# Where the low parts of u are made in an MLP's down projection, and how many of its pairs take seven products

## The chip, the cores and the metric

The kernel runs on one core of one Trainium2 chip. The metric is the device time of one execution in microseconds (us); the median of three runs of the kernel before is 1048.01 us. Five engines take part: TensorE (PE, its weight loads PEld), VectorE (DVE), ScalarE (ACT), GpSimd (POOL) and SyncE (SP). In this kernel SP only issues DMAs, POOL does so nearly always, and ACT hardly ever.

## The reference

One decoder layer on 256 positions of width 2048, in float32: two kinds of attention side by side, an output projection, and then the part that matters here, an MLP whose inner width is 8192:

```
h = _rmsnorm(x, norm_mlp_pre[layer])
u = jnp.square(jax.nn.relu(h @ w_up[layer]))
x = x + _rmsnorm(u @ w_down[layer], norm_mlp_post[layer])
```

`u` is 256 x 8192, `w_up` 2048 x 8192 and `w_down` 8192 x 2048.

## The kernel before

**Products in three passes.** PE multiplies numbers of a shortened float format (fp32r). To come near float32, each operand is split in two: `hi` is the number rounded to that format, which ACT makes with a copy (L306, or L310 with a gain), and `lo` is the rest, which DVE makes with a subtraction (L307, L311). A product is then three matmuls: hi by hi, hi by lo, lo by hi (`three`). Every weight is split once, as it comes in from HBM, in tiles of 128 x 1024; every activation is split too.

**Seven products.** For two neighbouring rows of weight tiles, a "pair" `kp`, the product of a 2 x 2 block of activations with a 2 x 2 block of weights may be formed with seven products of blocks in place of eight (`seven_products`), at the price of sums: DVE adds weight blocks (`sums` in `seven`, L361 to L366), and adds and subtracts activation blocks (`four_sums`, L977 to L979, called by `down_sums`). Some of the products go to accumulators of their own, `m`, which `close` adds up after the last pair of a stage. Of a pair with seven products four weight tiles are split (half a tile `b11`, and `b`, `u`, `t`); of a plain pair two.

**The up projection** goes through `w_up` in eight groups `j` of 1024 columns, each with 16 steps `k` over the rows; in all but the first group some pairs take seven products. The accumulators of a group are emptied while the next one runs (`up_evac`): Relu with the row's scale into a tile `r` (ACT, L937, two buffers), four transposes on PE, and a square into `uT[g]` (ACT, L949), 128 x 1024 numbers, one of 16 tiles `g` that lie in SBUF until the end. In the code's `up_evac` the tile's number is called `j`; two tiles come from each group of columns.

**The down projection** goes through `w_down` in two halves `c` of 1024 output columns. Each half has 32 pairs of rows, two to a tile of `u`. `DOWN_SEVEN` lists the pairs that take seven products: 8 in the first half and 13 in the second. The split of `u` (`split_u`) is made for one tile ahead, into `uhi` and `ulo`, two buffers each. In the first half ACT makes `uhi` and DVE `ulo`; each `ulo` is then stored to HBM (`keep_u`, SP's queue, L967), and the second half makes `uhi` again but loads `ulo` (POOL's queue, L960). For pairs that take seven products in both halves (`SHARED`), the split sums of `u`, called `s`, are stored in the first half (`keep_s`, L971) and loaded in the second (`down_back`, L404) in the same way.

**What sets the order.** The order is written out by hand. Each engine runs its instructions in the order in which the program emits them. `Weights` emits loads and splits of weights some six tiles ahead of the one in use, from a ring of eight buffers for `hi` and `lo`, and five for the raw tiles, which come in on SP's queue. Weights for pairs with seven products come in on POOL's queue, 1 MB at a time (L374): into `ab` and `ab2` by turns in the up projection, into `ab` and `c` in the first half of the down projection and into `ab` and `u01` in the second. `Flow` keeps a planner's clock that each matmul moves on by its nominal cost; a chain such as `up_evac` is a generator that gives the time until its next step, and `flow.pump()`, called after every three matmuls, emits the steps that are due. The delays in the code are times of that clock.

Of the kernel before, what the change touches and what calls it, by code (L numbers as in the profile page):

```python
# [18 lines left out]
F32 = mybir.dt.float32  # L19
F32R = mybir.dt.float32r  # L20
I32 = mybir.dt.int32
BF16 = mybir.dt.bfloat16
AF = mybir.ActivationFunctionType
OP = mybir.AluOpType
PSUM = bass.MemoryType.PSUM

P = 128
# [18 lines left out]
CW = 1024  # L46
# [55 lines left out]
def up_steps(first, *groups):  # L102
    steps = [("k", k) for k in first]
    for i, ks in enumerate(groups):
# [9 lines left out]
N_SEVEN = [sum(w == "w" for w, _ in steps) for steps in UP_STEPS]  # L114


DOWN_SEVEN = ((7, 11, 13, 17, 19, 23, 25, 29), range(3, 28, 2))
SHARED = [k for k in DOWN_SEVEN[0] if k in DOWN_SEVEN[1]]
GT = FF // 512
DOWN_STEPS = [[s for kp in range(2 * GT)  # L120
               for s in ([("w", kp)] if kp in ws else [("k", 2 * kp), ("k", 2 * kp + 1)])] for ws in DOWN_SEVEN]

# [141 lines left out]
def layer(nc, tc, io):  # L264
    flow = Flow()
# [8 lines left out]
    dram = tc.alloc_tile_pool(name="dram", bufs=1, space=bass.MemoryType.DRAM)  # L274
# [3 lines left out]
    def bank(i, name):  # L278
        return ps.tile([P, 512], F32, tag=f"bank{i}", bufs=1, name=name)
# [19 lines left out]
    def transpose(out, a):  # L299
        nc.tensor.transpose(out, a, ident)  # L300
        flow.spend(TR)

    def split(hi, lo, src, g=None):
        if g is not None:
            return split_gain(hi, lo, src, g)
        nc.scalar.activation(hi, src, AF.Copy)  # L306
        nc.vector.tensor_tensor(out=lo, in0=src, in1=hi.bitcast(F32), op=OP.subtract)  # L307
# [6 lines left out]
    def tok(t, k, b):  # L314
        return t[:, k, b * P:(b + 1) * P]
# [28 lines left out]
    late = {}  # L344
# [85 lines left out]
    def seven_down(c, kp):  # L430
        def load():

            n = DOWN_SEVEN[c].index(kp)
            raw = dpl["ab"]
# [246 lines left out]
    for half in range(2):  # L681
        qkv = {}
        for nms in (("qk", "v") if not half else "qkv"):
            accs = [acc for _, _, acc in proj(xT, [ch_a[half, nms]], f"{nms}{half}",
                                              bank_of=at_bank if (half, nms) == (0, "v") else None)]
            for i, nm in enumerate(nms):
                t = pa.tile([P, NB, 512], F32, tag=nm, name=f"{nm}_{half}")
# [215 lines left out]
    for ns in ((0, 1), (2,), (3,)):  # L903
# [4 lines left out]
        for c, b, acc in proj(mixT, [ch_o[n] for n in ns], f"o{ns[0]}", order, heads_done):  # L908
            n = ns[c]
            if not late:  # L910
# [8 lines left out]
                                  in_=io["norm_attn_post"].partition_broadcast(P).rearrange("p o d -> p (o d)"))  # L919
# [8 lines left out]
    hT = late["hT"]  # L928


    uT = {}

    def up_evac(j, b, i, acc, order):

        yield UP_STEP * order
        r = late["up"].tile([P, 512], F32, tag="r", bufs=2, name=f"r{j}_{b}")
        nc.scalar.activation(r, acc, AF.Relu, scale=rstd2[b])  # L937
        yield D_UP if j > 1 else 2 * D_UP
        t = bank(i, f"rt{j}_{b}")
        for k in range(4):  # L940
            transpose(t[:, k * P:(k + 1) * P], r[:, k * P:(k + 1) * P])
        if j not in uT:
            if j in (0, 1, 10, 11, 12, 13):
                t2 = late["u01" if j < 2 else "ab2" if j < 12 else "ab"][:, j % 2 * CW:(j % 2 + 1) * CW]
            else:
                tag = {"tag": "T", "bufs": 2} if j > 13 else {}
                t2 = late["up"].tile([P, CW], F32, name=f"uT{j}", **tag)
            uT[j] = t2.rearrange("p (k s) -> p k s", k=4)
        nc.scalar.activation(uT[j][:, :, b * P:(b + 1) * P], t.rearrange("p (k s) -> p k s", k=4), AF.Square)  # L949

    def split_u(c, g):
        if (c, g) == (0, 0):
            uh, ul = [wp.tile([P, CW], F32R, tag=w, bufs=W_BUFS, name=f"u{w}0").rearrange("p (k s) -> p k s", k=4)
                      for w in ("hi", "lo")]
        else:
            uh, ul = [dpl["dp"].tile([P, 4, S], F32R, tag=f"u{w}", bufs=2, name=f"u{w}{c}_{g}") for w in ("hi", "lo")]
        u, h, l = [x.rearrange("p k s -> p (k s)") for x in (uT[g], uh, ul)]
        if c and g:
            nc.scalar.activation(h, u, AF.Copy)
            nc.gpsimd.dma_start(out=l.bitcast(F32), in_=ukeep[g])  # L960
        else:
            split(h, l, u)
        return uh, ul

    def keep_u(g):
        ukeep[g] = dram.tile([P, CW], F32, name=f"ukeep{g}")
        nc.sync.dma_start(out=ukeep[g], in_=us[0, g][1].rearrange("p k s -> p (k s)").bitcast(F32))  # L967

    def keep_s(kp):
        st, skeep[kp] = skeep[kp], dram.tile([P, CW], F32, name=f"skeep{kp}")  # L970
# [50 lines left out]
    def seven_products(ts, left, accs, m, first, last, m_first=False):  # L1021

        (a11, a12, a22), (s3, s1, s2, s4) = left
        prods = ((a11, 0, 0, 1), (a12, 1, 0, (0, 0)), (s4, 1, 1, (0, 1)), (s2, 2, 0, 6), (a22, 2, 1, (1, 0)),
                 (s3, 3, 1, 7), (s1, 3, 0, 5))
        if m_first:
            prods = sorted(prods, key=lambda x: not isinstance(x[3], int))
        for p, (a, i, half, to) in enumerate(prods):
            w = weights.get(ts[i])
            in_m = isinstance(to, int)  # L1030
            three(m[to] if in_m else accs[to], a, [w[x][:, half * 512:half * 512 + 512] for x in range(2)],
                  in_m and first, in_m and last)
            if all(x[1] != i for x in prods[p + 1:]):
                weights.free(ts[i])
            flow.pump()

    def close(c, m):

        tt = nc.vector.tensor_tensor
        nc.scalar.activation(c[0], m[1], AF.Copy)  # L1040
        for out, x, y, op in ((1, m[6], c[0], OP.subtract), (2, m[7], c[1], OP.subtract),
                              (3, m[5], c[2], OP.subtract), (1, m[5], c[1], OP.add)):
            tt(out=c[out], in0=x, in1=y, op=op)
        return dict(zip(PARTS, c))

    def closing():
        return [late["c"][:, i * 512:(i + 1) * 512] for i in range(4)]
# [3 lines left out]
    for j in range(FF // CW):  # L1051
# [9 lines left out]
        for t, b in order:  # L1061
            what, k, tiles = steps[t]
# [9 lines left out]
            if (j, t, b) == (FF // CW - 1, 4, 0):  # L1072
                weights.limit -= 1
                u_next = split_u(0, 0)
# [6 lines left out]
            if what == "k":  # L1081
                w = weights.get(tiles[0])
                h_done(k, b)
                for n in range(2):
                    c = slice(n * 512, (n + 1) * 512)
# [28 lines left out]
    up = late["up"]  # L1114
# [5 lines left out]
    def down_mm(c, u, k, b, n, w, first, last):  # L1120
        three(y[b][2 * c + n], [tok(u[x], k % 4, b) for x in range(2)], [t[:, 0, n * 512:n * 512 + 512] for t in w],
              first, last)

    def spare(i, n):

        return uT[i + n // 2].rearrange("p k s -> p (k s)")[:, (n % 2) * 512:(n % 2) * 512 + 512]
# [66 lines left out]
    late["st"] = up.tile([P, ST], F32, tag="st", bufs=1, name="st_down")  # L1193
    dpl["ab"] = dp.tile([P, 2 * CW], F32, name="ab_down")

    us, ukeep = {(0, 0): u_next}, {}
    for c in range(2):

        for i, (b, n) in enumerate(PARTS):
            y[b][2 * c + n] = bank(4 * c + i, f"y{b}{2 * c + n}")  # L1200
        accs = {(b, n): y[b][2 * c + n] for b, n in PARTS}
        ws = DOWN_SEVEN[c]
        for t, (what, k, tiles) in enumerate(wide_d[c]):
            g = (2 * k if what == "w" else k) // 4
            u = us[c, g]
            if g >= GT - 2 and c:
                break
            if what == "k":
                w = weights.get(tiles[0])
                for b, n in PARTS:  # L1210
                    down_mm(c, u, k, b, n, w, t == 0, t == len(wide_d[c]) - 1)
                    flow.pump()
                weights.free(tiles[0])
            else:
                if k == ws[0]:
                    if not c:
                        flow.finish(*u_last)
                    else:
                        flow.finish(h_evac)
                    m = {i: bank(4 * (1 - c) + o, f"md{i}_{c}") for o, i in enumerate((1, 6, 7, 5))}  # L1220
                blocks = [[tok(u[x], 2 * (k % 2) + kk, bb) for x in range(2)] for kk, bb in ((0, 0), (1, 0), (1, 1))]
                seven_products(tiles, (blocks, left.pop((c, k))), accs, m, k == ws[0], k == ws[-1])
                if k == ws[-1]:
                    more = close([spare(10, i) for i in range(4)] if c else closing(), m)
                if not c and k in SHARED:
                    keep_s(k)
            nxt = (c, g + 1) if g < GT - 1 else (1, 0)
            if nxt not in us:
                if not c and g > 1:
                    keep_u(g - 1)  # L1230
                us[nxt] = split_u(*nxt)
            if (c, what, k) == (0, "k", 3):
                weights.limit += 1
            if (c, what, k) == (0, "k", 36):
                g_half = [late["up"].tile([P, 512], F32, tag="r", bufs=2, name=f"g_half{n}") for n in range(2)]
                for n in range(2):
                    load_gain(n, g_half[n])
            if (c, what, k) == (1, "k", 40):
                flow.start(x_back())
                for n in (2, 3):  # L1240
                    load_gain(n, spare(4, n))
        if not c:
            keep_u(GT - 1)
            h_evac = flow.start(half_evac(more, g_half))

    tail = {k: tiles[0] for what, k, tiles in wide_d[1] if k >= 4 * (GT - 2) and what == "k"}
    for g in (GT - 2, GT - 1):
        for b, n in PARTS:
            for kk in range(4):
                k = 4 * g + kk  # L1250
# [58 lines left out]
```

## Time and profile before

| what | value |
|---|---|
| median of three runs | 1048.01 us (1047.6 to 1048.62) |
| span of the profiled execution, first to last instruction | 1045.7 us |
| ACT, busy share of the span | 60% |
| POOL, busy share | 5% |
| HBM read, written | 212.72 MB, 15.73 MB |
| loads of weights for seven products on POOL's queue, to landing | `ab` 5.4 us, `ab_down` 7.1 us, `u` 8.4 us, `c` 8.9 us (median) |
| stores of `ulo`, to landing | 7.0 us (median of 15) |
| stores of `s`, to landing | 6.8 us (median of 7) |

The profiled execution's own time is this span and what lies around it, which the trace does not show. In the trace the up projection lies between about 354 and 701 us, the first half of the down projection between 701 and 871 us, and the second half ends at 1037 us. A line number such as L307 is a line of the kernel; since helpers record most operations, the tile names tell them apart. "Waited for" is idle time of an engine put down to what ended it. A row of groups gives the line, the engine, what is written from what, the count, the busy time in us, the mean in ns, and the idle time ahead of it.

### The profile page before, as it was taken

The page shows a single profiled execution, that of the slowest core. Times are in us where ns is not written, and L with a number is a line of the kernel's source. Part 1 is how long each engine was busy: PE and PEld are TensorE (multiplying, and loading weights), DVE is VectorE, ACT ScalarE, POOL GpSimd, SP SyncE. Part 2 cuts the span into 40 slices and gives each one's busy share as a digit, 9 for nine tenths or more (in the row PEclk, how much of TensorE's full clock was granted, in tenths as well). Part 3 has the DMA queues.
Part 4 walks back from the last instruction along what each step waited for, and adds up shares of the span by engine and source line. Part 5 has one row for each costly group of instructions (what it writes and reads, how often), then busy time and mean ns, then how long its engine had stood idle before and what let it go on. Part 6 is the DMA issues. An engine that isn't in the chain of part 4 may idle for free.

```text
span 1045.7 us, 13378 instructions
## 1 busy us (share of the span) xinstructions
PE 1035.7 (99%) x4837; PEld 863.2 (83%) x4837; DVE 838.7 (80%) x1122; ACT 630.4 (60%) x848; POOL 51.5 (5%) x83
## 2 busy tenths in 40 slices
PE   9999999999999999999999999999999999999996
PEld 6888889888888888888888888888888888888885
DVE  6676536567557669999999999897899978999995
ACT  6674436565545566665765667666567564766661
POOL 0000000000000000000000000000000000111100
PEclk9999999999999999999999999999999999999998
DMA  9975547454447295646657356378778767698952
GB/s 303 370 229 148 140 129 241 146 162 153 150 156 236 92 360 188 216 147 207 202 185 246 121 201 207 113 253 325 274 276 303 265 232 261 238 332 323 356 204 83
DMA packets 79938, 229.33 MB, mean 219 GB/s; under 512 B 6912, under 2 KB 11520, under 8 KB 79488
## 3 DMA queue, kind: packets, MB, share of 16 engines
q1 hardware_dynamic: 64576, 171.47, 48.9%
q0 software_dynamic: 14864, 56.63, 15.2%
q8 instruction: 38, 0.62, 0.3%
q10 hardware_dynamic: 432, 0.37, 0.1%
q14 instruction: 28, 0.23, 0.1%
HBM read 212.72 MB, written 15.73 MB: 218 GB/s over the span
## 4 chain that ended last, share of the span: by engine, by line
PE 97%; DVE 1%; issue 1%; ACT 0%; POOL 0%; DVEq 0%; POOLq 0%; ACTq 0%
PE y L296 25%; PE acc_u L296 24%; PE acc_o L296 8%; PE m L296 7%; PE md L296 5%; PE acc_qk L296 4%; PE acc_v L296 4%; PE acc_ckv L296 2%; PE acc_ukv L296 2%; PE acc_q L296 2%; PE acc_cq L296 2%; PE acc_k L296 2%; PE acc_uq L296 2%; PE rt L300 1%; PE sc_b L296 1%
## 5 line engine op out<-in xcount | busy, mean ns | idle before, releaser
L307 DVE TENSOR_TENSOR lo<-raw,hi 128x1024 fp32r<-128x1024 f32 (+3 forms) x213 | 241.5, 1152 | 89.8 <-ACT hi L306 89.1
L306 ACT ACTIVATE hi<-raw 128x1024 fp32r<-128x1024 f32 (+3 forms) x213 | 209.9, 999 | 73.6 <-PE y L296 16.1
L296 PE MATMUL y<-hi,uhi 128*128 128x512 f32 x370 | 144.4, 390 | 0.0
L296 PE MATMUL y<-hi,ulo 128*128 128x512 f32 x370 | 144.1, 389 | 0.0
L296 PE MATMUL y<-lo,uhi 128*128 128x512 f32 x370 | 144.0, 389 | 0.0
L296 PE MATMUL acc_u<-hi,hT_hi 128*128 128x512 f32 x356 | 141.7, 398 | 0.0
L296 PE MATMUL acc_u<-hi,hT_lo 128*128 128x512 f32 x356 | 139.2, 391 | 0.4 <-DVE hT_lo L307 0.4
L296 PE MATMUL acc_u<-lo,hT_hi 128*128 128x512 f32 x356 | 138.9, 390 | 0.0
L311 DVE SCALAR_TENSOR_TENSOR lo<-raw,gcol,hi 128x1024 fp32r<-128x1024 f32 x74 | 92.5, 1279 | 9.5 <-ACT hi L310 9.5
L310 ACT ACTIVATE hi<-raw,gcol 128x1024 fp32r<-128x1024 f32 x74 | 83.7, 1148 | 25.0 <-DMA raw<-in_w_up 11.7
L296 PEld LDWEIGHTS y<-hi,ulo 128*128 128x128 f32 x370 | 69.5, 188 | 14.4
L296 PEld LDWEIGHTS y<-lo,uhi 128*128 128x128 f32 x370 | 69.5, 188 | 14.3
L296 PEld LDWEIGHTS y<-hi,uhi 128*128 128x128 f32 x370 | 69.5, 188 | 14.2
L296 PEld LDWEIGHTS acc_u<-hi,hT_lo 128*128 128x128 f32 x356 | 66.8, 188 | 14.9 <-DVE hT_lo L307 0.8
L296 PEld LDWEIGHTS acc_u<-lo,hT_hi 128*128 128x128 f32 x356 | 67.0, 188 | 12.8
L296 PEld LDWEIGHTS acc_u<-hi,hT_hi 128*128 128x128 f32 x356 | 67.0, 188 | 12.8
L306 ACT ACTIVATE hi<-u 128x1024 fp32r<-128x1024 f32 (+1 forms) x38 | 37.4, 990 | 49.2 <-DVE u L366 35.4
L307 DVE TENSOR_TENSOR lo<-st_down,hi 128x1024 fp32r<-128x1024 f32 x42 | 50.4, 1220 | 3.0 <-ACT hi L306 2.8
L296 PE MATMUL acc_o<-hi,mixT_hi 128*128 128x512 f32 x128 | 51.8, 405 | 0.0
L306 ACT ACTIVATE hi<-st_down 128x1024 fp32r<-128x1024 f32 x42 | 43.9, 1052 | 12.6 <-PE y L296 9.5
L296 PE MATMUL acc_o<-hi,mixT_lo 128*128 128x512 f32 x128 | 50.2, 392 | 0.0
L296 PE MATMUL acc_o<-lo,mixT_hi 128*128 128x512 f32 x128 | 50.0, 391 | 0.0
(328 smaller groups left out, 2087.7 us busy)
## 6 DMA issues: line engine op xcount, KB each, us to landing
raw<-in_w_down SPq DMA_DIRECT2D x86, 512.0 KB, 5.8
raw<-in_w_up SPq DMA_DIRECT2D x76, 512.0 KB, 4.6
raw<-in_w_in SPq DMA_DIRECT2D x55, 512.0 KB, 4.9
ab<-in_w_up POOLq DMA_DIRECT2D x22, 1024.0 KB, 5.4
raw<-in_w_out SPq DMA_DIRECT2D x32, 512.0 KB, 4.2
ab_down<-in_w_down POOLq DMA_DIRECT2D x11, 1024.0 KB, 7.1
ukeep<-ulo SPq DMA_DIRECT2D x15, 512.0 KB, 7.0
ulo<-ukeep POOLq DMA_DIRECT2D x15, 512.0 KB, 6.2
```

The source lines that it names most:

```text
L296: nc.tensor.matmul(out, a, b, start=start, stop=stop)
L300: nc.tensor.transpose(out, a, ident)
L306: nc.scalar.activation(hi, src, AF.Copy)
L307: nc.vector.tensor_tensor(out=lo, in0=src, in1=hi.bitcast(F32), op=OP.subtract)
L310: nc.scalar.activation(hi, src, AF.Copy, scale=g)
L311: nc.vector.scalar_tensor_tensor(out=lo, in0=src, scalar=g, in1=hi.bitcast(F32), op0=OP.mult, op1=OP.subtract)
```

## The change

Three things change.

- The first half of the down projection takes seven products in eleven pairs: 5, 7, 9, 11, 15, 17, 19, 21, 25, 27 and 29, in place of 7, 11, 13, 17, 19, 23, 25 and 29. The second half's list stays. So ten pairs are in both lists, where there were seven: 5, 9, 15, 21 and 27 come in, 13 and 23 go out.
- The low part of `u` is made in HBM while the up projection runs, for tiles 1 to 15. As soon as both halves of a tile are there, a new chain, `lo_away`, is started with a delay of 5 (even tiles) or 12 (odd ones). For each 512 columns of the tile ACT makes a negated copy rounded to fp32r, which is minus `hi`, into a tile of the two buffers of `r`; ACT's own DMA queue stores it to HBM; and an accumulating DMA on POOL's queue adds the tile itself to it. What then stands in HBM is u - hi.
- So in the first half, too, `ulo` is loaded on POOL's queue for all tiles but the first, and neither DVE's subtraction nor the stores of `ulo` on SP's queue are there any more.

```diff
-DOWN_SEVEN = ((7, 11, 13, 17, 19, 23, 25, 29), range(3, 28, 2))
+DOWN_SEVEN = ((5, 7, 9, 11, 15, 17, 19, 21, 25, 27, 29), range(3, 28, 2))
...
-    uT = {}
+    uT, ukeep = {}, {}
...
         nc.scalar.activation(uT[j][:, :, b * P:(b + 1) * P], t.rearrange("p (k s) -> p k s", k=4), AF.Square)
+        if b and j:
+            flow.start(lo_away(j), 5.0 + 7.0 * (j % 2))
+
+    def lo_away(g):
+
+        ukeep[g] = dram.tile([P, CW], F32, name=f"ukeep{g}")
+        u = uT[g].rearrange("p k s -> p (k s)")
+        for h in range(2):
+            c = slice(h * 512, (h + 1) * 512)
+            t = late["up"].tile([P, 512], F32, tag="r", bufs=2, name=f"neg{g}_{h}")
+            nc.scalar.activation(t.bitcast(F32R), u[:, c], AF.Copy, scale=-1.0)
+            yield 1.0
+            nc.scalar.dma_start(out=ukeep[g][:, c], in_=t)
+            yield 9.0
+            nc.gpsimd.dma_start(out=ukeep[g][:, c], in_=u[:, c], accum_op=OP.add)
+            yield 2.0
...
-        if c and g:
+        if g:
             nc.scalar.activation(h, u, AF.Copy)
             nc.gpsimd.dma_start(out=l.bitcast(F32), in_=ukeep[g])
...
-    def keep_u(g):
-        ukeep[g] = dram.tile([P, CW], F32, name=f"ukeep{g}")
-        nc.sync.dma_start(out=ukeep[g], in_=us[0, g][1].rearrange("p k s -> p (k s)").bitcast(F32))
...
-    us, ukeep = {(0, 0): u_next}, {}
+    us = {(0, 0): u_next}
...
-                if not c and g > 1:
-                    keep_u(g - 1)
...
-            keep_u(GT - 1)
```

## The prediction

> **What bounds the kernel now.** I read the page first, then PE's waits, then the chain of waits, then the stages one by one.
>
> ```profile
> span 1045.7 us, 13378 instructions
> PE 1035.7 (99%) x4837; PEld 863.2 (83%) x4837; DVE 838.7 (80%) x1122; ACT 630.4 (60%) x848; POOL 51.5 (5%) x83
> PE warm L521 <- DVE zero L518: 1.2, 1, 1.2
> PE acc_u L296 <- DVE hT_lo L307: 0.4, 1, 0.4
> ```
>
> PE is busy in 1035.7 of 1045.7 us, and PE's waits list hardly anything: 1.2 us at the very start and 0.4 us once. No stage makes PE wait. So the count of matmuls sets the time, and a second engine matters only where it is about to make PE wait. The chain of waits gives what one matmul costs, and what lies behind the last one:
>
> ```profile
> 746.46 16.32 PE y L296 x72
> 1033.76 4.84 issue
> 1040.64 1.45 DVE uT L1151 x3
> ```
>
> 72 matmuls in 16.32 us are 0.2267 us each, the distance from start to start. (The 0.39 us that the page gives for one is its length; they overlap.) The end of the kernel, after the last matmul, is not touched by the change.
>
> The Trainium skill puts the sustained distance of 512-column matmuls at about 131 ns (TensorE: Matmul & The Clock Gate, Back-to-back issue gap); by it, an estimate, nine matmuls would be 1.18 us and the time 1046.8. This case's trace does not agree, with 226.7 ns and nothing waited for, so that time gets no chance.
>
> The table by stage (columns: window, its length, busy time and count of PE, PEld, DVE, ACT, POOL, then granted clock, DMA share, GB/s) shows who comes next:
>
> ```profile
> 572.70:615.40 42.70, 42.70 (x198) 35.38 (x197) 41.01 (x45) 28.08 (x33) 2.85 (x4) 1.00 0.54 188
> 780.00:820.00 40.00, 40.00 (x179) 33.11 (x178) 37.45 (x45) 23.68 (x26) 2.14 (x3) 1.00 0.85 304
> 920.00:970.00 50.00, 50.00 (x222) 41.44 (x221) 47.78 (x54) 33.07 (x37) 7.77 (x13) 1.00 0.92 337
> ```
>
> The first row is one group of the up projection: DVE is busy in 41.01 of 42.70 us, so it has 1.69 us to spare, while ACT has 14.6. The others are the two halves of the down projection. PE is full at clock 1.00 in all three.
>
> **The change part by part.** *Matmuls.* A pair as plain steps is 2 x 4 x 3 = 24 matmuls; by seven products it is 21. Eight pairs become eleven: 9 matmuls fewer, 9 x 0.2267 = 2.04 us, all on the path. Nothing else on PE changes.
>
> *First half, DVE.* The groups of 701 to 861 us:
>
> ```profile
> L306 ACT ACTIVATE hi<-raw 128x1024 fp32r<-128x1024 f32 x46 | 48.2, 1058 | 16.1 <-PE y L296 13.6 <-DMA raw<-in_w_down 1.4 <-ACT hi L306 0.8
> L307 DVE TENSOR_TENSOR lo<-raw,hi 128x1024 fp32r<-128x1024 f32 x46 | 55.5, 1220 | 10.9 <-ACT hi L306 10.9
> L307 DVE TENSOR_TENSOR ulo<-uT,uhi 128x1024 fp32r<-128x1024 f32 x10 | 12.2, 1221 | 3.8 <-ACT uhi L306 3.8
> L361 DVE TENSOR_TENSOR st_down<-ab_down 128x1024 f32<-128x1024 f32 x4 | 4.9, 1224 | 0.1
> L365 DVE TENSOR_TENSOR st_down<-st_down,ab_down 128x512 f32<-128x512 f32 x4 | 2.8, 692 | 0.1
> L307 DVE TENSOR_TENSOR lo<-c,hi 128x512 fp32r<-128x512 f32 x4 | 2.7, 685 | 0.0
> L977 DVE TENSOR_TENSOR st_down<-uT 128x256 f32<-128x256 f32 x6 | 2.5, 418 | 0.0
> L978 DVE TENSOR_TENSOR st_down<-st_down,uT 128x128 f32<-128x128 f32 x6 | 1.8, 292 | 0.2
> L307 DVE TENSOR_TENSOR s<-st_down,s 128x512 fp32r<-128x512 f32 x8 | 5.5, 686 | 0.0
> L306 ACT ACTIVATE s<-st_down 128x512 fp32r<-128x512 f32 x8 | 5.0, 631 | 10.0 <-DVE st_down L979 10.0
> ```
>
> Removed are 15 subtractions for ulo: 15 x 1.22 = 18.3 us. A pair by seven products takes weight sums of 1.22 + 2 x 0.69 = 2.60 us, splits of 3 x 1.22 + 0.69 = 4.35, sums of u of 0.42 + 2 x 0.29 = 1.00 and their split of 0.69: 8.64 us, in place of two plain splits (2.44). Three more pairs add 3 x 6.20 = 18.6 us. DVE comes out even, +0.3 us, and loses its peaks: a group of four k with a pair was 8.64 + 2.44 + 1.22 = 12.3 us of DVE in 45 matmuls (10.2 us of PE), and becomes 11.1. Both are a little high, since neighbours overlap (two of 1.22 us in a row take 2.35, a row further down shows), so the true figure lies between 10.6 and 11.1. Pairs 5 to 11 and 15 to 21 now make four such groups in a row, in which DVE falls behind by 4 x 0.4 to 4 x 0.9, that is 1.6 to 3.6 us; the group without a pair that follows needs 4 x 1.22 = 4.9 us of DVE for 10.9 of PE and makes up 6. The cover is the lead of the weights:
>
> ```profile
> 758.34 1.22 DVE L307 TENSOR_TENSOR lo<-raw,hi 128x1024 fp32r<-128x1024 f32 x1
> 767.61 0.39 PE L296 MATMUL y<-lo,uhi 128*128 128x512 f32 x1
> ```
>
> This is the first weight after pair 11, which follows a pair without a group between: done at 759.56, read at 767.61, 8 us ahead, and ACT waits 13.6 us in this half for buffers that PE has yet to free. Cost 0; without that lead up to 3.6 us a run of four would show.
>
> ACT gains 3 x (3 x 1.06 + 0.63 - 2 x 1.06 + 0.63) = 7.0 us in a half where it is busy in about 24 of 40: cost 0.
>
> *ulo from HBM.* In the first half POOL now issues 15 loads of 512 KB; the second half already runs so:
>
> ```profile
> DMA to landing us min/median/max: 4.2/6.2/8.8
> 914.07 0.55 POOL L404 DMA_DIRECT2D s<-skeep  x1 [8.03 <-PE md L296]
> 914.61 0.53 POOL L960 DMA_DIRECT2D ulo<-ukeep  x1
> ```
>
> (The first line is of L960, these loads.) A load can go once PE has left the buffer two groups back, which is when the group before its own begins, so it has 45 x 0.2267 = 10.2 us. The slowest took 8.8 (all in the second half, at its higher DMA share), and in the first half no load of s stands before it on POOL's queue. Behind it wait the loads of weight pairs, which are issued well ahead. Cost 0. SP loses 15 stores of ulo, 512 KB each, and gains three of s; the bytes of the half grow by 1.6 MB at a share of 0.85, which is under the 0.92 at which the second half keeps PE full. Cost 0.
>
> *Second half.* Pairs 5, 9, 15, 21 and 27 now load their s; 13 and 23 compute it again. At its start DVE is closest to PE:
>
> ```profile
> 881.01 0.41 DVE L977 TENSOR_TENSOR st_down<-uT 128x256 f32<-128x256 f32 x1
> 885.25 0.68 DVE L307 TENSOR_TENSOR s<-st_down,s 128x512 fp32r<-128x512 f32 x1
> 891.95 2.35 DVE L307 TENSOR_TENSOR lo<-raw,hi 128x1024 fp32r<-128x1024 f32 x2
> 893.41 0.39 PE L296 MATMUL y<-lo,uhi 128*128 128x512 f32 x1
> ```
>
> The first of the two lo is done near 893.2 and PE reads it at 893.41. The first two rows are pair 5's sums and split, which go: about 1.7 us of room. PE did not wait there, so nothing is gained.
>
> *Up projection.* Added are 30 negated copies of 128x512 on ACT, as many stores of 256 KB from its queue, and as many accumulating DMAs on POOL's, which add u to what was stored: four of each in a group of 42.7 us. A copy is 0.63 us (the s row). An issue on ACT's queue is in the trace only at the start:
>
> ```profile
> 29.53 0.34 ACTq L580 DMA_DIRECT2D pos_i<-in_pos  x1
> 29.90 0.45 ACTq L581 DMA_DIRECT2D cst<-in_consts  x1
> 588.89 1.15 ACT L310 ACTIVATE hi<-raw,gcol 128x1024 fp32r<-128x1024 f32 x1
> 593.33 1.06 ACT L306 ACTIVATE hi<-u 128x1024 fp32r<-128x1024 f32 x1 [1.69 <-DVE u L366]
> 593.13 1.28 DVE L311 SCALAR_TENSOR_TENSOR lo<-raw,gcol,hi 128x1024 fp32r<-128x1024 f32 x1
> 600.92 1.28 DVE L311 SCALAR_TENSOR_TENSOR lo<-raw,gcol,hi 128x1024 fp32r<-128x1024 f32 x1
> 605.51 0.39 PE L296 MATMUL acc_u<-lo,hT_hi 128*128 128x512 f32 x1
> ```
>
> Two issues took 0.79 us while ACT worked on an earlier instruction. A store must wait for its own copy, so I count 0.63 + 0.45 = 1.08 us of ACT for a half; the bounds are 0.63 (issue hidden) and, if copy, wait and issue stand in a row, some 1.5. By the planner's clock (0.65 us a step) the even tile's first copy falls some 15 us into a group, behind the splits for the second pair and ahead of a hi<-raw that ACT ends at 590.0 and DVE first reads at 593.13: 3.1 us of room, and behind it ACT idles 1.69 us for DVE's sums. The other three fall after similar points. So 1.08 us hides, and so does 1.5. Had DVE to wait all the same, the lo of k 14 is done at 602.2 and read at 605.51: 3.3 us ahead, about the least of a group. Cost 0.
>
> The copies also take turns with the Relu of L937 in the two buffers of r, so a Relu now waits until a store has landed. By the planner the last store of a group goes 38 us into it and the Relu that takes its buffer comes 7 us later. Even the slowest landing above, 8.8 us for twice the bytes, makes that Relu 1.8 us late, once a group, within the 3.3 us. Cost 0.
>
> The accumulating DMA is in no row. Its landing lies between 2.1 us (half of the quickest ulo load, for half the bytes) and some 18 (the slowest, twice over, for reading back and writing). It waits on POOL for the store to land; behind it stand loads of ab, for which DVE's sums of weights wait. The planner issues it 9 us behind the store, about the slowest landing, and loads of ab wait for DVE in any case:
>
> ```profile
> POOL ab L374 <- DVE lo L307: 254.3, 19, 29.2
> 588.65 0.71 POOL L374 DMA_DIRECT2D ab<-in_w_up  x1 [8.65 <-DVE lo L307]
> 598.34 1.22 DVE L361 TENSOR_TENSOR t<-ab 128x1024 f32<-128x1024 f32 x1
> ab<-in_w_up POOLq DMA_DIRECT2D x22, 1024.0 KB, 5.4
> ```
>
> The load at 588.65 lands near 594.1 and is read at 598.34: 4.2 us of room. It is issued 16 us into its group; the accumulation ahead of it is due at 7, so it may take 9 + 4 = 13 us before the sums are late. I take 6 us, near the loads of ulo, and so a cost of 0; four at 18 us in a group of 42.7 would not fit, and that is a rival. No wait goes that PE feels, so there is no gain either. Traffic rises by 2.1 MB a group (each byte once) to 4.2 (accumulated bytes three times), 49 to 98 GB/s on 188: at most 286, below the 304 and 337 above.
>
> **The sum.** 1045.7 - 2.04 = 1043.7 us of span. The median lies 2.3 us above that execution's span, so 1048.01 - 2.04 = 1045.97, say 1046.0 us.
>
> **Rivals.**
>
> *The second half gives it back.* With s and ulo in a row on POOL, ulo went at 914.61, 1.03 us after a group began (one began at 893.18, by the row of PE's lo less 0.23; two groups of 10.2 on is 913.58). 1.03 + 8.8 = 9.8 us of the 10.65 (a group, and two matmuls of the next) after which PE first reads ulo. Four pairs come to stand so (9, 15, 21, 27) and two (13, 23) cease to. If a further 512 KB at 337 GB/s, 1.55 us, comes on top, each is 0.7 us late: 4 x 0.7 = 2.9 us, 1048.9. For it: share 0.92 there. Against it: pairs 7, 11, 17, 19 and 25 stand so now and PE does not wait.
>
> *ACT sets the up projection's pace: slower.* Place: L306, L310 ahead of DVE's lo. If the halves fall where DVE needs hi at once, four cost 4 x 1.08 = 4.3 us a group; less DVE's 1.69, PE loses 2.6 us in each of six groups, less 3.3 of lead: 12.4, hence 1058.4. It decides from 0.42 us of delay a half. Against it: ACT's idle 14.6 us a group, and the room found above.
>
> *The accumulation is slow.* At over 42.7 / 4 = 10.7 us each the four fill POOL's queue for a whole group, and ab comes late. At 12 us: 5.3 us in six groups, 32 us, 1078. Nothing here shows such a rate for rows of 2 KB.
>
> **How the numbers follow.** Forecast 0.63, second half 0.18, ACT's pace 0.13, slow accumulation 0.04, the rest 0.02. A measurement of this kernel tells about 0.2%, 2.1 us, from no change, and the forecast is 2.04: its share that falls beyond 2.1 I put at four tenths, 0.25, with nothing from elsewhere. Slower takes the last three but a little of ACT's: 0.17. Within takes the rest: 0.58. Range: 1045.4 to 1049.0, the forecast and the second half, 0.81 in all (0.6 below for the spread of 1.0 us among the three runs); the likeliest case alone 1045.5 to 1046.6.
>
> **What would show it.** Right: nine matmuls fewer at 0.2267 us, the first half about 2 us shorter, no DVE or DMA among PE's waits, ulo of L307 gone from all but the first group, groups of the up projection still 42.7 us. Wrong: groups longer than 42.7 us with DVE waiting for ACT at L306 (ACT's pace), ab landing beyond 9 us (accumulation), PE waiting for ulo's DMA after 900 us (second half).

## The result and the profile after

The changed kernel takes **1056.5 us** (median of four runs, 1054.2 to 1058.33) and the kernel before 1047.8 (four runs, 1047.49 to 1048.62): a ratio of 1.0082, with a 95% interval of 1.007 to 1.0094. It is slower by 8.7 us; forecast was 1046.0, within 1045.4 to 1049.0.

The head of the page of the kernel after (span; then busy time, share and count of each engine):

```profile
span 1055.2 us, 13457 instructions
PE 1035.3 (98%) x4828; PEld 859.5 (81%) x4828; DVE 834.4 (79%) x1122; ACT 645.3 (61%) x884; POOL 90.0 (9%) x134
```

The counts are as worked out: nine matmuls fewer, DVE at 1122 instructions as before. The span is 9.5 us longer all the same, and with 2.0 us of matmuls gone about 11.5 us have been lost. Two of PE's waits in the kernel after are new (us in total, times, longest):

```profile
PE rt L300 <- ACT r L937: 9.2, 6, 1.8
PE acc_u L296 <- DVE c L1055: 0.4, 1, 0.4
```

Six times PE stands before the transposes of a finished up tile, because ScalarE's Relu (L937) is late. The table by stage of the kernel after says where (window, length, busy time and count of PE, PEld, DVE, ACT, POOL, granted clock, DMA share, GB/s):

```profile
444.60:487.30 42.70, 42.70 (x197) 35.34 (x196) 40.82 (x45) 29.58 (x37) 4.84 (x6) 1.00 0.75 229
487.30:530.00 42.70, 42.70 (x197) 35.36 (x196) 39.09 (x42) 29.51 (x37) 6.46 (x8) 1.00 0.76 234
530.00:572.70 42.70, 41.45 (x191) 33.99 (x190) 38.70 (x42) 27.40 (x34) 6.08 (x8) 1.00 0.79 232
572.70:615.40 42.70, 40.51 (x185) 32.69 (x184) 38.48 (x43) 28.33 (x37) 6.00 (x8) 1.00 0.73 219
615.40:658.10 42.70, 40.94 (x188) 33.29 (x187) 39.16 (x44) 28.35 (x37) 5.74 (x7) 1.00 0.76 225
658.10:700.80 42.70, 39.89 (x183) 32.53 (x182) 35.72 (x41) 25.48 (x33) 3.31 (x4) 1.00 0.65 200
700.80:740.00 39.20, 37.63 (x174) 30.81 (x174) 33.44 (x41) 28.10 (x37) 6.61 (x10) 1.00 1.00 349
740.00:780.00 40.00, 40.00 (x178) 33.14 (x177) 33.85 (x42) 26.70 (x32) 6.95 (x10) 1.00 0.95 313
```

Two groups of the up projection are whole, then PE is idle 1.25, 2.19, 1.76 and 2.81 us in a window of 42.7 (the lengths less PE's busy times), 1.57 at the start of the down projection, and nowhere later: 9.6 us. From start to start these seven stops cost more, 10.8 us in the trace, because the trace counts the matmul ahead of a stop with its whole length of 0.39 us and not 0.2267; where the last 0.7 us went was not settled. The up projection, from its first matmul to the first of the down projection, took 347.4 us before (354.12 to 701.56) and takes 357.3 now (353.81 to 711.06). In 530 to 701 us every window also has fewer matmuls than the 197 of a whole group. Clock and DMA share are no cause by themselves: the clock is 1.00, and PE is full at a DMA share of 0.95. Note that the loss begins late and repeats: it looks as if a lead were used up first, and then each group fell behind.

What the late groups have in common stands on POOL's queue. Its waits in 444 to 680 us, before:

```profile
POOL ab L374 <- DVE lo L307: 206.0, 17, 25.7
```

and after:

```profile
POOL ukeep L964 <- DMA ukeep<-neg: 126.9, 20, 10.5
POOL ab L374 <- DVE lo L307: 69.1, 10, 13.6
```

Before, POOL waited only for DVE to free a buffer of ab, so each load left at the first possible moment. Now it waits mostly for stores of negated tiles to land (to have their data written), with the loads behind it. The timeline of POOL's queue after (start, us, engine, line, operation, and the idle time before with what ended it):

```profile
560.73 0.88 POOL L964 DMA_DIRECT2D ukeep<-uT  x1 [6.94 <-DMA ukeep<-neg]
561.30 1.04 POOL L374 DMA_DIRECT2D ab<-in_w_up  x1
572.24 0.87 POOL L964 DMA_DIRECT2D ukeep<-uT  x1 [9.89 <-DMA ukeep<-neg]
581.47 0.85 POOL L964 DMA_DIRECT2D ukeep<-uT  x1 [8.36 <-DMA ukeep<-neg]
582.02 1.04 POOL L374 DMA_DIRECT2D ab<-in_w_up  x1
```

The last load is for the second pair of the next group. Before, it went 20 us earlier, and DVE read it 20 us later:

```profile
561.54 0.71 POOL L374 DMA_DIRECT2D ab<-in_w_up  x1 [7.08 <-DVE lo L307]
...
582.19 1.22 DVE L361 TENSOR_TENSOR t<-ab 128x1024 f32<-128x1024 f32 x1
```

DVE's waits for ab in 444 to 680 us in the kernel after (none before), and the one for this load:

```profile
DVE t L361 <- DMA ab<-in_w_up: 9.8, 4, 2.7
```

```profile
589.34 1.23 DVE L361 TENSOR_TENSOR t<-ab 128x1024 f32<-128x1024 f32 x1 [2.68 <-DMA ab<-in_w_up]
```

DVE has 1.69 us to spare in a group and now waits 2.68, so the next group starts late. ScalarE, in order, does the rest: its split of u waits for DVE's sums, and the second Relu stands behind that split, with PE's transposes behind the Relu. These rows are from the start of this group, which is late by such a wait in the group ahead:

```profile
577.90 0.69 ACT L937 ACTIVATE r<-acc_u,rstd_pre 128x512 f32<-128x512 f32 x1 [2.69 <-DVE acc_u L1121]
582.33 1.06 ACT L306 ACTIVATE hi<-u 128x1024 fp32r<-128x1024 f32 x1 [3.74 <-DVE u L366]
583.30 0.67 ACT L937 ACTIVATE r<-acc_u,rstd_pre 128x512 f32<-128x512 f32 x1
```

That second Relu came 4.4 us earlier before:

```profile
578.91 0.67 ACT L937 ACTIVATE r<-acc_u,rstd_pre 128x512 f32<-128x512 f32 x1
```

### The profile page after: what moved, and what is told of

Same layout as the page of the kernel before. It is cut to its first block, busy times and chain, and to the rows that moved or that the text cites. A ratio compares the mean times of both kernels' runs of the same rounds, so it can differ in the third digit from the quotient of the medians.

```text
span 1055.2 us, 13457 instructions
## 1 busy us (share of the span) xinstructions
PE 1035.3 (98%) x4828; PEld 859.5 (81%) x4828; DVE 834.4 (79%) x1122; ACT 645.3 (61%) x884; POOL 90.0 (9%) x134
## 4 chain that ended last, share of the span: by engine, by line
PE 78%; DVE 10%; DMA 6%; issue 3%; ACT 2%; POOL 0%; ACTq 0%; DVEq 0%; SPq 0%; POOLq 0%
PE y L296 24%; PE acc_u L296 11%; PE acc_o L296 8%; PE md L296 6%; PE acc_qk L296 4%; PE acc_v L296 4%; DVE lo L307 3%; PE m L296 3%; PE acc_ckv L296 2%; DVE lo L311 2%; DMA raw<-in_w_up 2%; PE acc_ukv L296 2%; PE acc_q L296 2%; PE acc_cq L296 2%; PE acc_k L296 2%
## 5 line engine op out<-in xcount | busy, mean ns | idle before, releaser
L307 DVE TENSOR_TENSOR lo<-raw,hi 128x1024 fp32r<-128x1024 f32 (+3 forms) x207 | 233.8, 1150 | 81.8 <-ACT hi L306 80.7
L306 ACT ACTIVATE hi<-raw 128x1024 fp32r<-128x1024 f32 (+3 forms) x207 | 203.4, 997 | 69.3 <-DMA raw<-in_w_in 14.4
L296 PE MATMUL acc_u<-hi,hT_hi 128*128 128x512 f32 x356 | 142.0, 399 | 0.4 <-DVE c L1055 0.4
L296 PE MATMUL acc_u<-hi,hT_lo 128*128 128x512 f32 x356 | 139.2, 391 | 0.4 <-DVE hT_lo L307 0.4
L296 PE MATMUL acc_u<-lo,hT_hi 128*128 128x512 f32 x356 | 138.8, 390 | 0.0
L296 PE MATMUL y<-hi,uhi 128*128 128x512 f32 x352 | 137.3, 390 | 0.0
L296 PE MATMUL y<-hi,ulo 128*128 128x512 f32 x352 | 137.0, 389 | 0.0
L296 PE MATMUL y<-lo,uhi 128*128 128x512 f32 x352 | 136.9, 389 | 0.0
L310 ACT ACTIVATE hi<-raw,gcol 128x1024 fp32r<-128x1024 f32 x74 | 82.9, 1145 | 27.8 <-DMA raw<-in_w_up 21.1
L296 PEld LDWEIGHTS acc_u<-hi,hT_lo 128*128 128x128 f32 x356 | 66.8, 188 | 15.2 <-DVE hT_lo L307 0.8
L296 PEld LDWEIGHTS acc_u<-hi,hT_hi 128*128 128x128 f32 x356 | 66.9, 188 | 14.1 <-DVE c L1055 1.4
L296 PEld LDWEIGHTS acc_u<-lo,hT_hi 128*128 128x128 f32 x356 | 67.0, 188 | 12.7
L296 PEld LDWEIGHTS y<-lo,uhi 128*128 128x128 f32 x352 | 66.1, 188 | 13.7
L296 PEld LDWEIGHTS y<-hi,ulo 128*128 128x128 f32 x352 | 66.1, 188 | 13.7
L296 PEld LDWEIGHTS y<-hi,uhi 128*128 128x128 f32 x352 | 66.1, 188 | 13.6
L306 ACT ACTIVATE hi<-u 128x1024 fp32r<-128x1024 f32 (+1 forms) x38 | 37.6, 991 | 61.1 <-DVE u L366 47.4
L307 DVE TENSOR_TENSOR lo<-st_down,hi 128x1024 fp32r<-128x1024 f32 x48 | 57.6, 1220 | 1.5 <-ACT hi L306 1.5
L306 ACT ACTIVATE hi<-st_down 128x1024 fp32r<-128x1024 f32 x48 | 50.0, 1050 | 3.5 <-DVE st_down L366 1.1
L296 PE MATMUL md<-hi,s 128*128 128x512 f32 x144 | 52.1, 389 | 0.0
L296 PE MATMUL acc_o<-hi,mixT_hi 128*128 128x512 f32 x128 | 51.8, 405 | 0.0
L296 PE MATMUL acc_o<-hi,mixT_lo 128*128 128x512 f32 x128 | 50.2, 392 | 0.0
```

The lines of the kernel that those rows point to most:

```text
L296: nc.tensor.matmul(out, a, b, start=start, stop=stop)
L310: nc.scalar.activation(hi, src, AF.Copy, scale=g)
```

## The experiments

**Theory A**: on POOL's queue, in order, an accumulation that waits for its store's landing holds the load of ab behind it. Rivals: **B**, ScalarE's copies and stores set the pace; **C**, the traffic alone makes the loads late; **E**, the eleven pairs cost by themselves.

### e1: accumulations issued later

```diff
-            yield 9.0
-            nc.gpsimd.dma_start(out=ukeep[g][:, c], in_=u[:, c], accum_op=OP.add)
-            yield 2.0
+            flow.start(add_u(g, c), 23.0)
+            yield 11.0
```

(add_u issues the same DMA.)

> All of the change stays (copies, stores, accumulating DMAs, eleven pairs); only the accumulating DMAs are issued 14 us later by the planner's clock, when their stores have long landed, and the copies and stores stay at their places. Theory A (on POOL's queue an accumulation waits for its store to land and holds the next load of ab behind it): no DVE wait at t<-ab, groups of the up projection back at 42.7 us, PE's waits at the transposes gone, 1046.0 us (1045.4 to 1047.5), ratio to before 0.998. Theory B (ScalarE's copies and stores set the pace): still 1056.5, with DVE waiting for hi. Theory C (the traffic alone makes the loads of ab late): still 1056.5, with ab landing in 8 us.

Measured: 1049.69 us (1047.99 to 1052.94); to before 1.0022 (1.0013 to 1.003). POOL's queue of e1:

```profile
553.75 0.74 POOL L374 DMA_DIRECT2D ab<-in_w_up  x1 [7.06 <-DVE lo L307]
554.49 0.95 POOL L954 DMA_DIRECT2D ukeep<-uT  x1
559.66 0.88 POOL L954 DMA_DIRECT2D ukeep<-uT  x1 [4.21 <-DMA ukeep<-neg]
561.54 0.74 POOL L374 DMA_DIRECT2D ab<-in_w_up  x1 [1.00 <-DVE lo L307]
```

The load leaves at 561.54 us, as before to the hundredth, and in 444 to 680 us DVE waits for ab no more. Nearly 7 of 8.7 us are back with every copy, store and accumulation still there: B falls, and so does most of C. Yet 1049.69 is above A's range. What is left of C shows in the last group. Landings of weight loads at 644 to 700 us (count, KB, median us), before:

```profile
raw<-in_w_up SPq DMA_DIRECT2D x7, 512.0 KB, 6.2
raw_w<-in_w_up SPq DMA_DIRECT2D x4, 512.0 KB, 4.0
```

and e1, where POOL's queue lets go several accumulations in a row there:

```profile
raw<-in_w_up SPq DMA_DIRECT2D x7, 512.0 KB, 8.8
raw_w<-in_w_up SPq DMA_DIRECT2D x4, 512.0 KB, 8.7
...
ukeep<-ab POOLq DMA_DIRECT2D x5, 256.0 KB, 9.2
```

At 640 to 745 us PE waits for the Relu twice in e1, 2.0 us in all. (The trace is of a run of 1048.47 us, below the median.)

### e2: the eleven pairs alone

The kernel before with the new list in DOWN_SEVEN and no other edit.

> The kernel before with the eleven pairs alone; ulo stays on VectorE. All theories on the low parts: the up projection is that of before. Rival E (the pairs themselves cost): above 1050, with PE waiting in the first half of the down projection. By the counts of before, DVE has 137.2 busy of 160 us in the first half and three pairs add 18.6: 155.8 of 158, so it just fits if it is spread evenly: 1045.8 to 1049, and 1046.5 taken.

Measured: 1050.11 us (1047.8 to 1051.83), 1.0019 (1.0009 to 1.0028). Above the value that I took, and above the range. The first half of e2, and its one new wait of PE in the down projection:

```profile
740.00:780.00 40.00, 40.00 (x178) 33.10 (x178) 39.55 (x47) 24.86 (x30) 2.15 (x3) 1.00 0.78 273
780.00:820.00 40.00, 40.00 (x178) 33.09 (x177) 39.52 (x47) 24.40 (x28) 2.15 (x3) 1.00 0.84 285
820.00:860.00 40.00, 40.00 (x179) 33.10 (x178) 39.59 (x45) 25.10 (x28) 1.43 (x2) 1.00 0.76 263
```

```profile
PE y L296 <- DVE lo L307: 2.1, 1, 2.1
```

DVE is busy 39.5 of 40 us throughout and reaches the second half without a lead; PE's wait falls there, not in the first half, where E had it. So without the low parts' relief the pairs cost more than their matmuls bring. The trace is of a run of 1048.21 us, where this one wait takes what the matmuls bring; six of the ten runs took 1049.99 us or more, and what they lost beyond it no trace shows.

### e3: the low parts alone

The kernel after with the eight pairs of before.

> The kernel after with the eight pairs of before. Theories A, B and C alike: the loss is all in the up projection and at the start of the down projection, the nine matmuls come back: 1056.5 + 2.0 = 1058.5 us (1057 to 1060). If the pairs cost by themselves (E): below 1056.

Measured: 1056.54 us (1055.52 to 1059.31), 1.0087 (1.0073 to 1.01). A miss by 2 us: with or without the pairs, the median is the same. That the nine matmuls bring nothing in the changed kernel does not follow: each of the two has four runs, some 4 us apart, and in the two traces the down projection (first matmul to last) is 0.8 us shorter with the eleven pairs (335.3 us, 336.1 in e3), while the up projection, whose loss is there without the pairs too, is 2.3 us longer (357.3, 354.9). Whether the pairs have a part in that was not settled.

### e4: no accumulating DMAs

```diff
-            nc.gpsimd.dma_start(out=ukeep[g][:, c], in_=u[:, c], accum_op=OP.add)
```

The kernel leaves out the sum: what it loads as ulo is minus hi, not u - hi.

> The kernel after without the 30 accumulating DMAs, so the low part of u is wrong in what is loaded; the 30 copies, 30 stores and 15 loads of ulo stay. Theory A: the loads of ab have nothing to stand behind: 1046.0 us (1045.4 to 1047). Theory B (copies and stores on ScalarE): 1056.5. Theory C (traffic): the stores' 256 KB each stay and the accumulations' go, so between, some 1050 to 1053.

Measured: 1047.39 us (1046.03 to 1048.76), 0.9996 (0.9987 to 1.0004). The 30 copies and stores stay, and the loss is gone: B falls a second time. A's value is missed by 0.4 us at the upper end.

### e5: one accumulation of four moved

```diff
-            yield 9.0
-            nc.gpsimd.dma_start(out=ukeep[g][:, c], in_=u[:, c], accum_op=OP.add)
-            yield 2.0
+            flow.start(add_u(g, c), 23.0 if h and g % 2 else 9.0)
+            yield 11.0
```

> As the kernel after, but of a group's four accumulating DMAs only one is issued later: that of the odd tile's second half, behind which the load for the next group's second pair stood. Theory A in its narrow form (this one load, held by this one wait): that load goes out by its buffer again, 8 us or more ahead, and nearly all of the loss goes: 1047 to 1050 us. If each of the four waits costs its share: one in four of the 8.8 us, so some 1054. Theories B and C: 1056.5.

Measured: 1049.28 us (1047.92 to 1050.13), 1.0015 (1.0006 to 1.0024). POOL's queue of e5:

```profile
566.92 0.87 POOL L954 DMA_DIRECT2D ukeep<-uT  x1 [6.29 <-DMA ukeep<-neg]
567.48 1.04 POOL L374 DMA_DIRECT2D ab<-in_w_up  x1
```

The second pair's load leaves at 567.48 instead of 582.02 us. It still stands behind a wait of 6.29 us, but that one ends early enough, and DVE no longer waits for ab in 444 to 680 us. One DMA in four moved brings 7.2 of 8.7 us: A in its narrow form. POOL's waits for stores are hardly shorter in all, 121.3 us instead of 126.9; what counts is which load stands behind which wait.

### e6 and e7: a version without the loss

e6: as e1, and 60.0 in place of 23.0 for tiles 10 to 15. e7: 14.0 in place of e6's 23.0.

> All of the change stays; accumulations 14 us later as in e1, and those of tiles 10 to 15 a further 37 us later, out of the last group of the up projection. What is left of e1's loss is 2.0 us of PE at the transposes of the last group, after raw loads of 6.7 to 9.0 us. Theory C in a small form (accumulations in flight together slow the raw loads there): that wait goes, profiled span about 1044.4, median 1047 to 1048 us. If something else makes the Relu late there (the new pair 5 at the start of the down projection): as e1, 1049.7.

> As e6, but the accumulations of tiles 1 to 9 only 5 us later than in the kernel after: then three of a group's four stand ahead of other loads than before, and the load for the next group's second pair still stands behind one of the odd tile's first half, whose store landed earlier. Theory A by the wait alone: as e6, 1047 to 1048, if the stores have landed by then (their landing is 3 to 8 us, the delay 14); if it still catches loads, 1049 to 1053.

Measured: e6 1047.58 us (1046.36 to 1049.55), 0.9999 (0.9991 to 1.0008); e7 1047.23 (1045.96 to 1049.78), 0.9997 (0.9988 to 1.0006). PE waits for no Relu in either. The same landings in e6:

```profile
raw<-in_w_up SPq DMA_DIRECT2D x7, 512.0 KB, 6.4
raw_w<-in_w_up SPq DMA_DIRECT2D x4, 512.0 KB, 5.7
...
ukeep<-ab POOLq DMA_DIRECT2D x1, 256.0 KB, 8.7
```

One accumulation instead of five beside them, and they are nearly as quick as before: C in its small form. These raw loads go on SP's queue, so POOL's order does not hold them.

### e8: e6 with the eight pairs

> As e6 with the eight pairs of before: the low parts by themselves, with their harm removed. By the matmuls, 2.0 us more than e6: 1049 to 1050; if the low parts by HBM gain nothing and cost nothing, 1047.7, as before. If the eleven pairs still cost something by themselves after e6's relief of VectorE, it is no slower than e6.

Measured: 1047.95 us (1047.48 to 1049.29), 1.0004 (0.9995 to 1.0013). With the harm removed, the low parts neither cost nor bring anything that the runs can tell. The pairs bring 0.4 (e6) to 0.7 us (e7, which has other delays than e8) in the medians, less than the runs of one kernel differ, where 2.04 were due.

### e9, e10, e11: where the nine matmuls' gain stays

e9 is e7 with one line more in half_evac, which empties the first half's banks; e10 has that line alone on the kernel before; e11 is e9 with a twelfth pair, 13.

```diff
                 square(n, b)
+                yield 1.0
                 yg[n, b] = out
```

> e7, and in the emptying of the first half's banks one step of 1 us more between ScalarE's square and VectorE's product with the gain, which had waited four times 0.8 us in order behind it. In e7 PE waits once in the down projection, at 892.95 us for a lo of VectorE, whose chain from the closing sums at 862 us is full. Theory F (the nine matmuls' gain is taken back there, since VectorE's chain did not move with PE's): PE's wait for lo goes, 1046.5 us or less (1046.0 by the sum of the prediction, up to 1047). If the wait there is no part of it: 1047.2, as e7.

> The kernel before with the step of e9 alone: a control. PE waits for nothing there, so by every theory 1047.8 us, as before; were it faster, e9's gain would not speak for the pairs.

> e9 with a twelfth pair (13) by seven products in the first half: three matmuls fewer, 0.68 us. VectorE has some 146 busy of 158 us there and gets 6.2 more, 152. If it fits: 0.7 us under e9, 1045.3 to 1046.3. If VectorE's lead into the second half goes: as e9 or up to 2 us slower.

Measured: e9 1047.36 us (1046.01 to 1050.21), 0.9998 (0.9989 to 1.0007); e10 1048.15 (1047.33 to 1048.9), 1.0 (0.9991 to 1.0008); e11 1046.89 (1045.87 to 1049.35), 0.9995 (0.9986 to 1.0003). DVE's chain from the closing sums (c<-md) to the splits of raw weights at 892 us, in e6, with what PE waits for there:

```profile
862.09 2.87 DVE L1058 TENSOR_TENSOR c<-md,c 128x512 f32<-128x512 f32 x4
891.71 1.22 DVE L307 TENSOR_TENSOR lo<-raw,hi 128x1024 fp32r<-128x1024 f32 x1
```

```profile
PE y L296 <- DVE lo L307: 1.0, 1, 1.0
```

and its start before, whose end at 891.95 the prediction shows:

```profile
861.16 2.87 DVE L1043 TENSOR_TENSOR c<-md,c 128x512 f32<-128x512 f32 x4
```

Nine matmuls bring PE there about 2 us earlier than before, DVE is 0.24 earlier. In e9 that wait of PE is gone, as theory F has it, but its time is missed: another took its place.

```profile
PE y L296 <- DMA ulo<-ukeep: 0.7, 1, 0.7
```

POOL's queue of e9 ahead of it (the wait falls at 960 to 990 us):

```profile
963.97 0.55 POOL L404 DMA_DIRECT2D s<-skeep  x1 [8.44 <-PE md L296]
964.51 0.53 POOL L979 DMA_DIRECT2D ulo<-ukeep  x1
965.03 0.70 POOL L374 DMA_DIRECT2D ab_down<-in_w_down  x1
```

That is the prediction's rival for the second half, s and ulo in a row, with 0.7 us, though once and not four times. e11 lies above the value for a twelfth pair that fits: its trace, of its slowest run, has PE waiting 1.2 us at 891.67 us for DVE's c (L1198), at the same boundary. The medians of e7, e9 and e11 can't be told from before's, so no version was shown to beat it.

The traces tell more than the medians, because they separate the stages. From the start of its first matmul to the start of its last, the down projection took 335.6 us before (701.56 to 1037.14), 335.6 in e8, 335.4 in e6, 334.5 in e7 (702.32 to 1036.81) and 334.6 in e9: about 1.0 of the 2.04 us is there once the stop for DVE is down to 0.6 us (e7) or gone (e9, with the 0.7 us for ulo). Ahead of the up projection, which the change leaves alone, the traces differ as much: its first matmul starts at 354.12 us before, 354.73 in e7, 354.91 in e10 and 355.61 in e11.

### e12: the loads of ab on SP's queue

```diff
-            return load_two(late[UP_PAIRS[j][kp]], nc.gpsimd if (j, kp) > (1, 0) else nc.sync,
+            return load_two(late[UP_PAIRS[j][kp]], nc.sync,
```

> The kernel after with one edit: the loads of ab in the up projection go by SP's queue, among the raw loads, and POOL's queue keeps only the accumulating DMAs at their places. Theory A: a store's landing holds no load any more, so the loss goes as in e5 or more: 1047 to 1050 us, no DVE wait at t<-ab for more than 1 us. Against it, a rival of the same kind on the other queue: SP is in order too, a load of ab waits there up to 14 us for VectorE to free its buffer, and raw loads stand behind it: then ACT and DVE wait for raw loads, and the time is 1056 or more. Theories B and C: 1056.5.

Measured: 1055.45 us (1053.57 to 1056.89), 1.0073 (1.0059 to 1.0087): A's number is missed, and the rival's nearly met. SP's waits of e12 in 444 to 680 us, and what ACT meets:

```profile
SPq L374 <- DVE lo L307: 145.8, 17, 18.8
```

```profile
613.28 1.15 ACT L310 ACTIVATE hi<-raw,gcol 128x1024 fp32r<-128x1024 f32 x1 [6.60 <-DMA raw<-in_w_up]
```

No row of DVE there waits for ab. But loads of ab now stand on SP's queue until DVE frees their buffers, raw loads stand behind them, and ACT waits for those. The wait has moved to the neighbouring queue. How much of it is order and how much the raw loads' slower landing (7.3 us in the median, 4.3 before) was not told apart.

## Why the prediction was wrong

**The step that failed** is the accumulating DMA's wait: "behind it stand loads of ab ... and loads of ab wait for DVE in any case", hence "a cost of 0". Two things were wrong in it. The room was that of another load: the one shown there, at 588.65 us, had 4.2 us of room, but which load stands behind which accumulation was not worked out. The load that counts had 20 us from its issue at 561.54 to its use at 582.19, and two waits in a row (9.89 and 8.36 us) with their issues took all of it. And the wrong landing was priced: the 6 us were the accumulation's own, which holds nothing on POOL's queue (the load at 582.02 leaves 0.55 us behind an accumulation), while the store's landing, which does hold it, was taken as covered by the 9 us of planner's clock between the two. The store that counts left ScalarE 11 us after the load had gone in the kernel before:

```profile
572.77 0.33 ACTq L962 DMA_DIRECT2D ukeep<-neg  x1
```

What waits for it starts at 581.47, 8.7 us later. By e5 this one wait, once a group, is worth 7.2 of 8.7 us, by e4 all accumulations together 9.1.

**Matmuls**: nine fewer came (4828), but the 2.04 us did not. In the changed kernel the last late Relu, a stop of 1.57 us in the down projection, takes most of it; once the late Relus are mended, 0.4 to 0.7 us show in the medians and 1.0 to 1.1 in the down projection of the traces of e7 and e9. At the start of the second half DVE's chain was rightly named as closest to PE, but that "pair 5's sums and split" go was taken for relief enough: in e6 the chain is 1.2 us shorter (29.6 for 30.8) and begins 0.9 later. Why it began later was not settled.

**First half, DVE even**: right, 1122 instructions in both. DVE has 139.0 busy of 160 us in the first half, 137.2 before. e2 shows what the relief is worth: without it DVE is at 99%.

**Copies and stores on ScalarE hidden**: right (e4, e8). A copy took 0.62 us and its issue 0.33, against 1.08 us allowed for both.

**Relu and copies sharing buffers, 3.3 us of lead**: no Relu waited for a store. The place was named in part: the Relu is where the lead runs out, but through ScalarE's order (the split of u ahead of it waits for DVE), not through buffers.

**The rivals**: the slower one, ScalarE's pace, did not occur. Of its two signs the groups were longer than 42.7 us, but DVE's wait for ACT at L306 in 444 to 680 us fell from 7.6 to 6.1 (at L310 it rose from none to 2.5, where ACT itself waits 9.0 us for raw loads). The slow accumulation was the right place, with the wrong price: "ab landing beyond 9 us" was not needed, since ab landed in 8.0 us there in the median. Time went in the wait ahead of the issue, which no landing shows. A sign should have been "loads of ab issued later than before". The second half's cost did not occur in the changed kernel, where PE waits for nothing after 740 us; it showed in e9, 0.7 us once.

The Trainium skill says that accumulating in a DMA is open to GpSimd's path alone, while plain transfers may go from SP or ScalarE (DMA: Bandwidth & Descriptors, SWDGE vs HWDGE vs iDMA). The traces agree as far as they go: all 30 accumulations are POOL's, and plain loads ran from SP in e12. By that rule the accumulation cannot leave the queue here, only what stands behind it can. The Trainium skill also fits a GpSimd DMA by 2.0 us and 436 KB per us (DMA: Bandwidth & Descriptors, Anatomy of one DMA — SWDGE (gpsimd) path), an estimate of 2.6 us for 256 KB and 4.4 for 1024; the runs show 4.7 us for accumulations from uT and 8.0 for loads of ab at 444 to 680 us, and 5.4 for these loads before. The measurement decides: the estimate is too short for these transfers, beside the other queues' traffic here.

## What to carry to other kernels

When a DMA that waits for another transfer goes on a queue, write down the loads that the planner puts behind it, one by one, ask when the transfer that it waits for is itself issued, and compare each load's room with the sum of the waits ahead of it, not with one landing. Issue such a DMA when what it waits for has long landed: 14 us more of delay gave back 6.8 of 8.7 us here (e1), and spreading the last ones the rest (e6). And follow a gain of matmuls to the next stage boundary: if the next engine's chain does not move with PE, the gain shrinks there, as by 0.6 us in e7 and 1.2 in e11.

## What was not expected of the hardware

Accumulating DMAs close together went with slower landings. With three let go between 647.63 and 650.35 us (e1), raw_w landed in 8.7 us in 644 to 700 us, against 4.0 before, 5.0 with no accumulation (e4) and 7.1 in the kernel after, which spreads as many out; the accumulations themselves took 9.2, against 5.6 in the kernel after. That their being together is the cause was not shown: the single one of e6 took 8.7. POOL's issue of an accumulation took 0.85 to 0.95 us against 0.71 for a plain load, and a plain load right behind one took 1.04. Most of the changed kernels spread more from run to run than the kernel before (e1 1047.99 to 1052.94, e3, with eight pairs, 1055.52 to 1059.31, before 1047.18 to 1049.22 on the same chip). Only one execution of each has a trace. Part of the difference lies ahead of the up projection: there PE waits for ACT's splits (acc_qk L296 <- ACT hi L306) 0.3 to 1.5 us in e1, e2, e6, e7, e9, e10 and e11, and not in before. Why stays open.
